# A DRAM-to-DRAM copy of 32 MB on one core: eight transfers of 32 KB per partition, or two of 128 KB

## The chip, the cores and the metric

The kernel runs on one core of a Trainium2 chip. The metric is device time in microseconds (us) from launch to end; the median of several executions is compared. One execution was also recorded by the hardware profiler. Its span is the time from the first to the last instruction of the core, and its device time is a little longer than that span.

## The reference: what is computed

```python
batch, seq, hidden, capacity = 16, 1024, 512, 256
x = np.random.randn(batch, seq, hidden).astype(np.float32)
token_positions = np.random.randint(0, capacity, (batch, seq))

mask = token_positions < capacity
return (x * mask[..., np.newaxis]).astype(np.float32)
```

Rows of `x` (one per token, 512 floats, 2 KB) are kept where the token's position is below the capacity and set to zero elsewhere. The positions are drawn from 0 to 255 and the capacity is 256, so with these inputs every row is kept and the output equals `x`: 16,384 rows, 33.55 MB in and 33.55 MB out.

## The kernel before, in words

The 16,384 rows are seen as 128 groups ("partitions") of 128 consecutive rows each. One partition is 256 KB of consecutive bytes in DRAM, in `x` as in the output.

**The copy.** The kernel copies `x` to the output at once, from DRAM to DRAM, without waiting to know whether a row has to be dropped. The loop at L78 to L83 issues the copy in transfers. Transfer k takes `C` rows of each partition, rows k*C to (k+1)*C, so with C = 16 (L77) there are eight transfers, each with a run of 32 KB from every one of the 128 partitions, 4,096 KB in all. Even k goes to the queue of SP (the SyncE engine), odd k to the queue of ACT (ScalarE). So each queue has four transfers. Each adds 16 to the semaphore `s_copy` when it has landed. No transfer waits for another: the issuing engine only hands it over and goes on.

**The order of issue.** L72 issues a load of the token positions (`tp`, 128 KB, 1 KB per partition) on ACT's queue, ahead of ACT's copies. L86 to L95 take these nine DMA instructions out of the block where they were written and put them ahead of SP's first instruction of the program's first block, so that they are the first thing that SP and ACT do.

**The check beside it.** The positions are 64-bit integers, seen as a low and a high 32-bit half. VectorE (DVE) waits for `tp` (L102), compares the halves (L103 to L115) into a keep flag per row, and adds the flags along each partition (L119). TensorE adds the 128 partial sums with one product with ones (L123). L125 makes one integer of it: 1 if fewer than 16,384 rows are kept. SP, ACT and DVE read that integer into a register (L133) and branch on it.

**The repair.** Within the branch (L141 to L162) the rows would be loaded again, multiplied by the flags and stored, after a wait for all of `s_copy`. With these inputs the integer is 0 and the branch isn't taken.

**The end.** SP, ACT and DVE report to GpSimd (POOL), which clears the semaphores and then waits for the whole copy. That wait, `gp.wait_ge(s_copy, 16 * n_copy)`, with `n_copy` counted by the loop, is the last one of the program.

The functions in full, with the line numbers of the profile:

Of the kernel before, what the change touches and what calls it, by code (L numbers as in the profile page):

```python
# [1 line left out]

# [4 lines left out]


@with_exitstack
def kernel(  # L10
    ctx: ExitStack,
    tc: tile.TileContext,
    x: bass.AP,
    token_positions: bass.AP,
    capacity: bass.AP,
    out: bass.AP,
):
    nc = tc.nc
    P = nc.NUM_PARTITIONS
    fp32 = mybir.dt.float32  # L20
    i32 = mybir.dt.int32
    Alu = mybir.AluOpType

    x_f = x.flatten_outer_dims()
    out_f = out.flatten_outer_dims()
    N, D = x_f.shape
    n_per_p = N // P
    cap = float(int(capacity))
    x_r = x_f.rearrange("(p n) d -> p n d", p=P)
    out_r = out_f.rearrange("(p n) d -> p n d", p=P)  # L30
    tp_i32 = token_positions.rearrange("b s -> (b s)").bitcast(i32)

    sp = nc.sync
    act = nc.scalar
    ve = nc.vector
    pe = nc.tensor
    gp = nc.gpsimd


    tc.close()  # L40
    tc.compile()  # L41

    def sbuf(name, shape, dtype):
        return ctx.enter_context(nc.sbuf_tensor(name, shape, dtype)).ap()

    tp = sbuf("tp", [P, 2 * n_per_p], i32)
    ge = sbuf("ge", [P, n_per_p], fp32)
    lt = sbuf("lt", [P, n_per_p], fp32)
    low = sbuf("low", [P, n_per_p], fp32)
    keep = sbuf("keep", [P, n_per_p], fp32)  # L50
    kept = sbuf("kept", [P, 1], fp32)
    ones = sbuf("ones", [P, 1], fp32)
    drop_i = sbuf("drop_i", [1, 1], i32)
    total = ctx.enter_context(nc.psum_tensor("total", [1, 1], fp32)).ap()
    F = 16
    NBUF = 2
    n_fix = n_per_p // F
    xts = [sbuf(f"xt{b}", [P, F, D], fp32) for b in range(NBUF)]

    s_copy = nc.alloc_semaphore("s_copy")  # L60
    s_tp = nc.alloc_semaphore("s_tp")
    s_ve = nc.alloc_semaphore("s_ve")
    s_pe = nc.alloc_semaphore("s_pe")
    s_ld = [nc.alloc_semaphore(f"s_ld{b}") for b in range(NBUF)]
    s_mul = nc.alloc_semaphore("s_mul")
    s_st = [nc.alloc_semaphore(f"s_st{b}") for b in range(NBUF)]
    s_done = nc.alloc_semaphore("s_done")

    n_copy = 0
    early = []  # L70

    load_tp = act.dma_start(out=tp, in_=tp_i32.rearrange("(p w) -> p w", p=P))  # L72
    early.append(load_tp.then_inc(s_tp, 16).ins)

    C = 16  # L77
    for k in range(n_per_p // C):  # L78
        ins = (sp, act)[k % 2].dma_start(
            out=out_r[:, k * C : (k + 1) * C, :], in_=x_r[:, k * C : (k + 1) * C, :]  # L80
        ).then_inc(s_copy, 16)
        early.append(ins.ins)
        n_copy += 1  # L83


    home = nc.cur_bb.bb  # L86
    first_bb = nc.cur_f.blocks[0]
    first_sp = next(
        k for k, i in enumerate(first_bb.instructions) if i.engine == mybir.EngineType.SP
    )  # L90
    names = [i.name for i in early]
    home.instructions = [i for i in home.instructions if i.name not in names]
    first_bb.instructions = (
        first_bb.instructions[:first_sp] + early + first_bb.instructions[first_sp:]
    )  # L95

    lo = tp[:, 0 : 2 * n_per_p : 2]
    hi = tp[:, 1 : 2 * n_per_p : 2]


    ve.memset(ones, 1.0).then_inc(s_ve, 1)  # L101
    ve.wait_ge(s_tp, 16)  # L102
    ve.tensor_scalar(  # L103
        out=ge, in0=lo, scalar1=0.0, scalar2=None, op0=Alu.is_ge
    ).then_inc(s_ve, 1)
    ve.wait_ge(s_ve, 2)
    ve.scalar_tensor_tensor(  # L107
        out=lt, in0=lo, scalar=cap, in1=ge, op0=Alu.is_lt, op1=Alu.mult
    ).then_inc(s_ve, 1)
    ve.wait_ge(s_ve, 3)  # L110
    ve.scalar_tensor_tensor(  # L111
        out=low, in0=hi, scalar=0.0, in1=lt, op0=Alu.is_equal, op1=Alu.mult
    ).then_inc(s_ve, 1)
    ve.wait_ge(s_ve, 4)
    ve.scalar_tensor_tensor(  # L115
        out=keep, in0=hi, scalar=0.0, in1=low, op0=Alu.is_lt, op1=Alu.add
    ).then_inc(s_ve, 1)
    ve.wait_ge(s_ve, 5)
    ve.tensor_reduce(  # L119
        out=kept, in_=keep, axis=mybir.AxisListType.X, op=Alu.add  # L120
    ).then_inc(s_ve, 1)
    pe.wait_ge(s_ve, 6)
    pe.matmul(out=total, lhsT=ones, rhs=kept, start=True, stop=True).then_inc(s_pe, 1)  # L123
    ve.wait_ge(s_pe, 1)
    ve.tensor_scalar(  # L125
        out=drop_i, in0=total, scalar1=float(N) - 0.5, scalar2=None, op0=Alu.is_lt
    ).then_inc(s_ve, 1)


    for e in (sp, act, ve):  # L130
        e.wait_ge(s_ve, 7)
    ET = mybir.EngineType
    drop = nc.values_load(  # L133
        drop_i[0:1, 0:1],
        engines=[ET.SP, ET.Activation, ET.DVE],
        min_val=0,
        max_val=1,
        skip_runtime_bounds_check_because="a comparison gives 0 or 1",
    )
    with nc.If(drop):  # L140
        for u in range(n_fix):  # L141
            b = u % NBUF
            if u >= NBUF:
                sp.wait_ge(s_st[b], 16 * (u // NBUF))
            sp.dma_start(out=xts[b], in_=x_r[:, u * F : (u + 1) * F, :]).then_inc(s_ld[b], 16)
            ve.wait_ge(s_ld[b], 16 * (u // NBUF + 1))
            for j in range(F):
                c = u * F + j
                ve.tensor_scalar(
                    out=xts[b][:, j, :],  # L150
                    in0=xts[b][:, j, :],
                    scalar1=keep[:, c : c + 1],
                    scalar2=None,
                    op0=Alu.mult,
                ).then_inc(s_mul, 1)
            if u == 0:
                act.wait_ge(s_copy, 16 * n_copy)
            act.wait_ge(s_mul, (u + 1) * F)
            act.dma_start(out=out_r[:, u * F : (u + 1) * F, :], in_=xts[b]).then_inc(s_st[b], 16)
        for b in range(NBUF):  # L160
            act.wait_ge(s_st[b], 16 * (n_fix // NBUF))


    for e in (sp, act, ve):
        e.sem_inc(s_done, 1)
    gp.wait_ge(s_done, 3)
    own = [s_tp, s_ve, s_pe, *s_ld, s_mul, *s_st, s_done]
    ids = sorted(s.num for s in own)
    assert ids == list(range(ids[0], ids[-1] + 1))
    gp.sem_clear(range(ids[0], ids[-1] + 1))  # L170
    gp.wait_ge(s_copy, 16 * n_copy)
    gp.sem_inc(s_copy, -16 * n_copy)


# [1 line left out]
_INS = ['x', 'token_positions', 'capacity']  # L176
_OUTS = [((16, 1024, 512), 'float32')]

_NUMBERS = {'capacity': 256}


# [26 lines left out]
```

## Time and profile before

| What | Value |
|---|---|
| median of 4 runs | 105.22 us (104.95 to 105.36) |
| device time of the profiled execution | 105.01 us |
| its span | 103.1 us |
| device time around the span (105.01 - 103.1) | 1.9 us |
| DVE busy | 1.5 us, 7 instructions |
| PE busy | 0.2 us |
| POOL busy | 0.2 us |
| last instruction of the check (L125) starts | 6.49 us |
| issue of SP's four copies | 0.0 to 3.0 us |
| issue of ACT's load and four copies | 0.13 to 3.3 us |

How to read the profile of this kernel: issuing a DMA, waiting for a semaphore and branching aren't counted as busy time, so an engine whose row is empty may be issuing or waiting. The work is in the DMA rows. "DMA" is the mean busy share of the core's 16 DMA engines, in tenths for each of 40 slices of the span. "GB/s" counts the bytes of the packets that begin in a slice, so with large packets it swings from slice to slice although the flow is even. Bytes are counted once, on their way from source to destination; the line on HBM (the DRAM) counts reads and writes apart. A packet is one piece of a transfer that one DMA engine carries. The queue q1 is SP's and q10 is ACT's (it also carries the `tp` load).

### The profile page before, as it was taken

To read this page: it belongs to the slowest core of one execution; us is meant where nothing else is said; L and a number is where in the kernel's file an instruction comes from. 1 tells how busy PE (TensorE), PEld (TensorE's weight loads), DVE (VectorE), ACT (ScalarE), POOL (GpSimd) and SP (SyncE) were. 2 spreads that over 40 slices of the span, in tenths; PEclk is the share of its full clock that TensorE was granted. 3 is DMA by queue.
4 is the path that set the end of the run, shared out by engine and by line. 5 is a ranking of instruction groups with operands and counts; after the bars stand their busy time and mean duration, and the time that the engine had idled before them with its cause. 6 is when DMAs were issued, how large, how long until landed. Compare 5 with 4: busy or idle time off the path is not lost. (4 is left out here: it accounts for less than half of the span.)

```text
span 103.1 us, 70 instructions
## 1 busy us (share of the span) xinstructions
PE 0.2 (0%) x2; PEld 0.1 (0%) x2; DVE 1.5 (1%) x7; POOL 0.2 (0%) x4
## 2 busy tenths in 40 slices
PE   0000000000000000000000000000000000000000
PEld 0000000000000000000000000000000000000000
DVE  0140000000000000000000000000000000000000
POOL 0000000000000000000000000000000000000000
DMA  7998999989989999799798999898997998998974
GB/s 254 407 381 292 330 283 330 343 292 369 343 292 394 305 318 407 254 356 356 254 407 305 305 407 318 292 369 292 356 356 254 407 330 280 369 343 305 394 254 165
DMA packets 1297, 33.69 MB, mean 327 GB/s; under 512 B 144, under 2 KB 272, under 8 KB 272
## 3 DMA queue, kind: packets, MB, share of 16 engines
q10 hardware_dynamic: 720, 16.91, 49.5%
q1 hardware_dynamic: 576, 16.78, 48.2%
q14 instruction: 1, 0.01, 0.0%
HBM read 33.69 MB, written 33.55 MB: 652 GB/s over the span
## 5 line engine op out<-in xcount | busy, mean ns | idle before, releaser
L115 DVE SCALAR_TENSOR_TENSOR keep<-tp,low 128x128 f32<-128x128 int32 x1 | 0.3, 292 | 0.0
L107 DVE SCALAR_TENSOR_TENSOR lt<-tp,ge 128x128 f32<-128x128 int32 x1 | 0.3, 291 | 0.0
L111 DVE SCALAR_TENSOR_TENSOR low<-tp,lt 128x128 f32<-128x128 int32 x1 | 0.3, 291 | 0.0
L119 DVE TENSOR_REDUCE kept<-keep 128x1 f32<-128x128 f32 x1 | 0.3, 286 | 0.0
L103 DVE TENSOR_SCALAR ge<-tp 128x128 f32<-128x128 int32 x1 | 0.2, 227 | 0.0
L123 PE MATMUL total<-kept,ones 128*1 128x1 f32 x2 | 0.2, 164 | 6.3 <-DVE kept L119 6.3
L125 DVE TENSOR_SCALAR drop_i<-total 1x1 int32<-1x1 f32 x1 | 0.1, 145 | 0.3 <-PE total L123 0.3
L101 DVE MEMSET ones<- 128x1 f32 x1 | 0.1, 59 | 4.7 <-PEq L41 4.7
L189 POOL MEMSET const-bfloat16-1.0<- 128x1 bf16 x1 | 0.1, 101 | 0.0
L189 POOL MEMSET const-uint8-127<- 128x1 uint8 x1 | 0.1, 101 | 0.0
L189 POOL MEMSET const-float32-0.0<- 128x1 f32 x1 | 0.1, 98 | 0.2 <-issue 0.2
L189 POOL MEMSET const-float32-1.0<- 128x1 f32 x1 | 0.1, 98 | 0.0
L123 PEld LDWEIGHTS total<-kept,ones 128*1 128x1 f32 x2 | 0.1, 80 | 6.3 <-DVE kept L119 6.3
## 6 DMA issues: line engine op xcount, KB each, us to landing
out_dram<-in_x_dram SPq DMA_DIRECT2D x4, 4096.0 KB, 61.5
out_dram<-in_x_dram ACTq DMA_DIRECT2D x4, 4096.0 KB, 67.2
tp<-in_token_positions_dram ACTq DMA_DIRECT2D x1, 128.0 KB, 2.1
```

The lines of the kernel that those rows point to most:

```text
L101: ve.memset(ones, 1.0).then_inc(s_ve, 1)
L103: ve.tensor_scalar(out=ge, in0=lo, scalar1=0.0, scalar2=None, op0=Alu.is_ge).then_inc(s_ve, 1)
L107: ve.scalar_tensor_tensor(out=lt, in0=lo, scalar=cap, in1=ge, op0=Alu.is_lt, op1=Alu.mult).then_inc(s_ve, 1)
L111: ve.scalar_tensor_tensor(out=low, in0=hi, scalar=0.0, in1=lt, op0=Alu.is_equal, op1=Alu.mult).then_inc(s_ve, 1)
L115: ve.scalar_tensor_tensor(out=keep, in0=hi, scalar=0.0, in1=low, op0=Alu.is_lt, op1=Alu.add).then_inc(s_ve, 1)
L119: ve.tensor_reduce(out=kept, in_=keep, axis=mybir.AxisListType.X, op=Alu.add).then_inc(s_ve, 1)
L123: pe.matmul(out=total, lhsT=ones, rhs=kept, start=True, stop=True).then_inc(s_pe, 1)
L125: ve.tensor_scalar(out=drop_i, in0=total, scalar1=float(N) - 0.5, scalar2=None, op0=Alu.is_lt).then_inc(s_ve, 1)
L189: nc = _bacc.Bacc("TRN2", target_bir_lowering=False, num_devices=1)
```

## The change

The constant `C` becomes 64. The loop then makes two transfers instead of eight: SP copies rows 0 to 63 of every partition and ACT rows 64 to 127, so that each transfer takes 128 KB of each partition's 256 KB, 16,384 KB in all. `n_copy` becomes 2, and the waits on `s_copy` are for 32 instead of 128.

```diff
-    C = 16
+    C = 64
     for k in range(n_per_p // C):
         ins = (sp, act)[k % 2].dma_start(
             out=out_r[:, k * C : (k + 1) * C, :], in_=x_r[:, k * C : (k + 1) * C, :]
```

In the built program a transfer of before is 128 runs of 8,192 floats (32 KB). A transfer of the changed kernel is 128 times 2 runs of 16,384 floats (64 KB): the 128 KB of a partition are cut in two. Every other instruction, and the order of all of them on PE, DVE and POOL, is the same; on SP and ACT one copy instruction stands where four stood.

## The prediction

> **What bounds the kernel now.** I read the page's engine rows first, then its DMA rows, then the chain, then the time windows, and at last the DMA view of the two ends.
>
> ```profile
> span 103.1 us, 70 instructions
> PE 0.2 (0%) x2; PEld 0.1 (0%) x2; DVE 1.5 (1%) x7; POOL 0.2 (0%) x4
> ...
> DMA  7998999989989999799798999898997998998974
> ...
> DMA packets 1297, 33.69 MB, mean 327 GB/s; under 512 B 144, under 2 KB 272, under 8 KB 272
> ## 3 DMA queue, kind: packets, MB, share of 16 engines
> q10 hardware_dynamic: 720, 16.91, 49.5%
> q1 hardware_dynamic: 576, 16.78, 48.2%
> ...
> HBM read 33.69 MB, written 33.55 MB: 652 GB/s over the span
> ## 4 chain that ended last, share of the span: by engine, by line
> DVE 2%; issue 0%; PE 0%
> ```
>
> No engine computes for more than 1.5 us, and the DMA row is near nine tenths from the first slice to the last but two. The chain names only the check (2% of the span): it ends in the first 7 us, and the copy, which really ends last, isn't in it because its end is a semaphore and no instruction. So the copy is the bound. The packets tell how it is cut: eight copies of 128 pieces plus 16 completion packets, the `tp` load the same, and one for instructions: 9 x 144 + 1 = 1297. Per queue, 576 = 4 x 144. The two shares add up to 97.7%, or 100.7 of 103.1 us: the 16 DMA engines hardly ever rest.
>
> ```profile
> 1.60:102.70 101.10, 0.19 (x2) 0.09 (x2) 1.53 (x7) 0.00 (x0) 1.00 0.99 333
> ...
> 6.00:26.00 20.00, 0.19 (x2) 0.09 (x2) 0.36 (x2) 0.00 (x0) 1.00 0.99 326
> 26.00:46.00 20.00, 0.00 (x0) 0.00 (x0) 0.00 (x0) 0.00 (x0) 1.00 1.01 338
> 46.00:66.00 20.00, 0.00 (x0) 0.00 (x0) 0.00 (x0) 0.00 (x0) 1.00 0.99 329
> 66.00:86.00 20.00, 0.00 (x0) 0.00 (x0) 0.00 (x0) 0.00 (x0) 1.00 0.99 329
> ```
>
> The last two numbers of each window are the DMA share and GB/s. Between the first piece of the copy (1.6 us; in the DMA view one packet of q1 begins just before 1.62) and its end (102.7 us) the engines are 99% busy at 333 GB/s, and every 20 us look alike. A busy engine isn't an engine at full speed, though, as the start shows:
>
> ```profile
> DMA packets 120, 1.63 MB, mean 400 GB/s; under 512 B 16, under 2 KB 72, under 8 KB 72
> q1 hardware_dynamic: 48, 1.57, 103.2%
> q10 hardware_dynamic: 72, 0.06, 4.2%
> ```
>
> That is the DMA view from 1.6 to 5.68 us: 48 pieces of the copy, three per engine, all from SP's queue. 1.57 MB in 4.08 us is 385 GB/s. So the same engines with the same pieces have gone 16% faster than their mean; what holds them to 333 GB/s later is outside of them, most likely the memory that they all read and write (652 GB/s both ways over the span). The Trainium skill, page "HBM Reference", section "Specifications (TRN2)", gives about 716 GB/s for a domain's DRAM; by that the copy's 67.1 MB would need at least an estimated 93.7 us in whatever pieces, and no run here shows that limit.
>
> **The change part by part.**
>
> 1. *Pace of the copy: 0.* The bytes, the 16 engines, the two queues and the 256 KB pitch of the partitions stay. The pieces become 64 KB, and the two queues work 128 KB apart in a partition instead of 32 KB. Which addresses are open at one time is thus new, and no row shows its price. Bounds from the 20 us windows: at 326 GB/s all through, 101.1 x 333/326 is 103.3 us, +2.2; at 338 it is 99.6, -1.5. Part of that spread is counting (a round of 16 pieces is 0.52 MB, 26 GB/s of a window). I take 0, the mean.
>
> 2. *Gaps between packets: -0.1.* Each engine has 64 copy pieces and 8 completion packets; it will have 32 and 2. 72 packets become 34. The engines' idle time within the 101.1 us is 1% at most, 1.0 us, and 0.4 us of that is the uneven end (part 4). The rest, 0.6 us, is 8 ns per packet; 38 packets fewer would give -0.3 us, if the engines and not the memory set the pace. Bounds 0 and -0.3; I take -0.1.
>
> 3. *Start: +0.3.* The issue instructions:
>
> ```profile
> L79 SPq DMA_DIRECT2D out_dram<-in_x_dram x4: 582/626/1045, 0.0 to 2.4; - x4
> L79 ACTq DMA_DIRECT2D out_dram<-in_x_dram x4: 581/638/791, 0.6 to 2.5; - x4
> ```
>
> (ns, shortest, median, longest; then first and last start.) SP's first issue, of 128 pieces, starts at 0.0; data flows at 1.6. The one issue now has 256 pieces. If issue time doesn't depend on their number, nothing changes; if it doubles and the data waits for all of it, the cost is +1.05 us, the longest row. The `tp` load has 128 pieces as well and took 393 ns (timeline), so the number of pieces isn't all; I take +0.3, half of a median issue. The six issues that go are worth nothing: they run from 0.6 to 3.3 us, beside data that is already flowing. The `tp` load is still first on ACT's queue; if a 64 KB piece got ahead of it, the check would end some 3 us later than now (one piece at 20.8 GB/s per engine, 333/16, is 3.15 us). It ends at 6.6 us, so 96 us of copy cover that. The branch and POOL's last wait stay as they are.
>
> 4. *End: 0.* The 16 completion packets of ACT's last transfer all lie between 101.9 and 102.8 us in the DMA view: the engines end within some 0.8 us of each other. Each still carries 2 MB. While some have ended, the rest have the memory to themselves and may speed up, as at the start. Bounds: 0, and +1.6 if one engine ends half a new piece (32 KB, 1.57 us) late.
>
> *Semaphores: 0.* Six fewer completions; nobody waits for the single ones, only POOL for the sum.
>
> Sum against the profiled execution: 105.01 + 0 - 0.1 + 0.3 + 0 = 105.2. That execution is 0.2 below the median of 105.22, so on the median the forecast is **105.4 us**, no change that a measurement of this kernel could tell (about 0.3%, or 0.3 us).
>
> A rule that speaks against this change is in the Trainium skill, page "Perfetto Trace Analysis", section "DMA Optimizations": smaller transfers may let some begin sooner. By that the start term would stand at its upper end, and the sum at about 106.0 instead of 105.2; the trace shows only that 1.6 us pass before the first data and can't say how much of it goes with the number of pieces.
>
> **The rivals.**
>
> - *The end frays (slower): 106.2 to 107.0.* An engine can't hand a piece to another. With pieces twice as long the engines may end twice as far apart: +0.8 us, up to +1.6 with one engine half a piece late. For it: the last two slices already fall to 7 and 4 tenths, and in the last 4 us only ACT's queue has work, so nothing fills gaps. Against: every engine has the same 2 MB, and the late ones may speed up. It decides from the point where the spread of the 16 last completions exceeds about 1.2 us.
> - *The memory likes the new addresses less (slower): 106.5 to 107.6.* Half or all of +2.2 from part 1. For it: the pace already varies between 385 and 326 GB/s with nothing but addresses and engine phases changing. Against: the 20 us windows, between which the transfers move through the whole partition, differ by few per cent.
> - *The fast start lasts longer, or the pace is better (faster): 103.9 to 104.8.* The first three pieces per engine came from SP's queue alone, at 385 GB/s. Three pieces of 64 KB would take twice as long; if they keep that pace, the second half gains 4.08 x (385/333 - 1) = 0.6 us: 104.8. With the better pace of part 1 instead, 105.4 - 1.5 = 103.9. Against: from 97.9 to 101.4 us ACT's queue is alone too, at 328 GB/s in the window, so being alone isn't what made the start fast.
> - *Nothing changes in what the engines see*, if pieces are cut to 32 KB again on the way: the forecast's own time.
>
> **How the numbers follow.** Forecast (with the last rival): 0.38. Fraying end 0.20, worse addresses 0.17: together 0.37 slower. Faster: 0.25, since the start shows that there is pace to be had, but nothing in the change reaches for it. The range takes in the bounds of the rivals, 103.9 to 107.6; some 0.15 is left out, for two costs that come together and for prices that no row shows. The forecast's own range is 104.9 to 105.5.
>
> **What would show it.** Packets: 2 x (256 + 16) + 144 + 1 = 689, q1 with 272 and q10 with 416; more means that the pieces are cut again. The start: the first q1 packet at about 1.9 us instead of 1.6. Pace: 333 GB/s within 1% in the long windows; 326 or less is the address rival. End: a spread of the last 16 completions of about 0.8 us; over 1.2 is the fraying end. The fast start: pieces of q1 alone from 1.6 to about 10 us at over 370 GB/s would be the faster rival. The forecast is wrong if the pace moves by more than 1%, since each per cent is 1.0 us and every other term is below that.

## The result and the profile after

The changed kernel takes 105.51 us (median of 44 runs, 105.08 to 106.1) against 105.12 us before (70 runs, 104.66 to 105.73). The ratio is 1.0039, with a 95% interval of 1.003 to 1.0049: slower by 0.4 us. The profiled execution took 105.6 us with a span of 103.7; that of before took 105.01 with 103.1.

The page of the changed kernel, in the lines that answer to those shown of before:

```profile
span 103.7 us, 64 instructions
...
DMA  9994999859999759999399999299994899992990
...
DMA packets 689, 33.69 MB, mean 325 GB/s; under 512 B 48, under 2 KB 176, under 8 KB 176
## 3 DMA queue, kind: packets, MB, share of 16 engines
q10 hardware_dynamic: 416, 16.91, 49.2%
q1 hardware_dynamic: 272, 16.78, 48.6%
...
HBM read 33.69 MB, written 33.55 MB: 648 GB/s over the span
```

The packets are the 689, 272 and 416 that two transfers in 64 KB pieces give, so nothing cuts the pieces again. The two shares add up to 97.8%, as before within a tenth: of the longer span that is 101.4 us busy, against 100.7. The time isn't in gaps between packets (2.3 us of rest against 2.4); the same bytes keep the engines busy 0.7 us longer. The low digits in the DMA row come from counting: a packet is put down to the slice in which it begins, and a piece of 64 KB now lasts longer than a slice (about 2.9 us in the first pieces, against 2.6).

The time windows of before (first fence) and after (second fence), last two numbers DMA share and GB/s:

```profile
1.50:7.20 5.70, 0.19 (x2) 0.09 (x2) 1.53 (x7) 0.00 (x0) 1.00 1.06 390
...
30.00:60.00 30.00, 0.00 (x0) 0.00 (x0) 0.00 (x0) 0.00 (x0) 1.00 1.00 333
60.00:90.00 30.00, 0.00 (x0) 0.00 (x0) 0.00 (x0) 0.00 (x0) 1.00 1.00 331
```

```profile
1.50:7.20 5.70, 0.19 (x2) 0.09 (x2) 1.54 (x7) 0.00 (x0) 1.00 1.07 385
...
30.00:60.00 30.00, 0.00 (x0) 0.00 (x0) 0.00 (x0) 0.00 (x0) 1.00 0.99 330
60.00:90.00 30.00, 0.00 (x0) 0.00 (x0) 0.00 (x0) 0.00 (x0) 1.00 1.00 330
```

No stretch stands out. A difference of 1 to 3 GB/s is below what such a window can show: one round of 16 pieces of 64 KB is 1.05 MB, 35 GB/s of a 30 us window. So windows of one trace cannot place 0.4 us, and the experiments have to.

Issue of the copies, in the changed kernel (ns, shortest, median, longest):

```profile
L79 SPq DMA_DIRECT2D out_dram<-in_x_dram x1: 694/694/694, 0.0 to 0.0; - x1
L79 ACTq DMA_DIRECT2D out_dram<-in_x_dram x1: 643/643/643, 0.6 to 0.6; - x1
```

SP's issue of 256 pieces took 694 ns. Before, its first issue of 128 pieces took 619 ns (the longest, 1045 ns, was its third), and in e2 and e8 below one issue of 512 and one of 2,048 pieces took 617 ns each. The number of pieces isn't what an issue costs.

### The profile page after: what moved, and what is told of

The parts are those of the page before. It is cut to its first block, busy times and chain, and to the rows that moved or that the text cites. A ratio compares the mean times of both kernels' runs of the same rounds, so it can differ in the third digit from the quotient of the medians.

```text
span 103.7 us, 64 instructions
## 1 busy us (share of the span) xinstructions
PE 0.2 (0%) x2; PEld 0.1 (0%) x2; DVE 1.5 (1%) x7; POOL 0.2 (0%) x4
## 6 DMA issues: line engine op xcount, KB each, us to landing
out_dram<-in_x_dram ACTq DMA_DIRECT2D x1, 103.1
```

## The experiments

Each kernel is compared with before on its own chip, where before had a median of 106.35 us (first four runs), 106.40 us (next four) or 105.16 us (last four). Ratios are to before, as recorded; they are not quite the quotients of the medians. The diffs are against the changed kernel unless said otherwise.

**First question: the size of the pieces, the number of transfers, or the end?** Theory P puts the cost on pieces of 64 KB, theory N on having two transfers only, theory F on engines that end further apart when the pieces are long.

Run e1, four transfers in 64 KB pieces:

```diff
-    C = 64
+    C = 32
```

> C = 32: four transfers, two on each queue, in pieces of 64 KB. Theory P (the pieces of 64 KB cost the time, however many transfers they are in) expects the changed kernel's time, ratio to before about 1.004, and the 16 last completions spread over about 1.0 us. Theory N (what costs is that two transfers alone remain, each walking through half a partition before it goes on to the next) expects a ratio of 1.000 to 1.002.

Measured: 106.75 us, ratio 1.0028 (1.0004 to 1.0051). The trace has 721 packets, and the 16 last completions lie 1.0 us apart.

Run e2, two transfers in 32 KB pieces:

```diff
-    C = 64
+    C = 16
+    xq = x_r.rearrange("p (h q c) d -> p q h (c d)", q=2, c=C)
+    oq = out_r.rearrange("p (h q c) d -> p q h (c d)", q=2, c=C)
+    for q, e in enumerate((sp, act)):
+        ins = e.dma_start(out=oq[:, q], in_=xq[:, q]).then_inc(s_copy, 16)
```

(In place of the loop over k; the last two lines of that loop stay. SP takes the even 32 KB of a partition, ACT the odd ones.)

> Two transfers, one on each queue, in pieces of 32 KB: SP takes the even 32 KB of every partition and ACT the odd ones. Theory P (piece size) expects the time of before, ratio 1.000, and 0.8 us of spread at the end. Theory N (two transfers, partition by partition) expects 1.004.

Measured: 106.44 us, ratio 1.0002 (0.9973 to 1.003), and a spread of 1.17 us at the end. Two transfers as such cost nothing that can be seen, and four in long pieces are slower: this speaks for P and against N, although the two intervals overlap (the medians are 0.31 us apart). The spread was expected at 0.8 us and is larger than the changed kernel's 1.05, without a longer time. That is the first mark against F. The changed kernel's spread is read from the view of 102.28 to 103.34 us, which just holds its 16 completion packets:

```profile
DMA packets 16, 0.00 MB, mean 0 GB/s; under 512 B 16, under 2 KB 16, under 8 KB 16
q10 hardware_dynamic: 16, 0.00, 0.8%
```

One thing goes with the size of the pieces in these runs and wasn't taken apart from it: how far apart in a partition the two queues work. It is 32 KB in before and in e2, 64 KB in e1 and 128 KB in the changed kernel.

Run e3, small pieces at the end:

```diff
+    for e, n in [(sp, 64), (act, 48), (act, 4), (act, 4), (act, 4), (act, 4)]:
```

> As the changed kernel, but ACT's half ends in small pieces: 48 rows in one transfer, then four transfers of 4 rows (8 KB pieces). Theory F (the loss is at the end, where engines with long pieces end further apart) expects 0.3 to 0.4 us back, ratio about 1.000 to 1.001, and a spread of the last completions of about 0.8 us or less. If the spread has nothing to do with the size of the last pieces, 1.004 and about 1.0 us.

Measured: 106.69 us, ratio 1.003 (1.0006 to 1.0054). The 16 completions lie within 0.88 us, and nothing is gained. The views from 103.65 to 104.54 us and from 104 us on show all 16 completions, and that four engines had theirs before 104:

```profile
DMA packets 31, 0.12 MB, mean 138 GB/s; under 512 B 16, under 2 KB 16, under 8 KB 16
```

```profile
DMA packets 16, 0.03 MB, mean 55 GB/s; under 512 B 12, under 2 KB 12, under 8 KB 12
```

Run e4, the same end on the kernel before:

```diff
+    for e, n in [(sp, 16), (act, 16), (sp, 16), (act, 16), (sp, 16), (act, 16), (sp, 16), (act, 4), (act, 4), (act, 4), (act, 4)]:
```

> As before (pieces of 32 KB), but the last 16 rows on ACT go in four transfers of 4 rows (8 KB pieces). Theory F expects the end to fray less here too: 0.2 to 0.4 us faster than before, ratio 0.996 to 0.998. If the spread at the end is not set by the pieces, 1.000.

Measured: 106.57 us, ratio 1.0017 (0.999 to 1.0043): no gain. But the completions still lie 0.82 us apart, against 0.77 before, so the small pieces didn't make the engines end together, and this run doesn't test F. Against F stand e2, with a wide end and no loss, and e3, which ends nearly as evenly as before and stays slow. What a quite even end would be worth, no run shows.

**Second question: is it lost at every piece, or once per launch?** Two runs make the copy four times (three times to spare tensors), so what is lost per megabyte counts four times and what is lost at the two ends counts once. Both have the same code, e5 with `C = 16` and e6 with `C = 64`:

```diff
+    spare = [
+        nc.dram_tensor(f"spare{r}", [N, D], fp32).ap().rearrange("(p n) d -> p n d", p=P)
+        for r in range(3)
+    ]
+    for to in [*spare, out_r]:
+        # ... the loop over k, with `to` in place of `out_r`
```

> The copy of before (C = 16) made four times, three times to spare DRAM tensors and then to the output: four times the bytes behind one start and one end. It is the base of the next run. Every theory expects 105.1 + 3 x 101 = some 408 us if the pace of the copy stays, about 3.88 times before.

> The copy of the changed kernel (C = 64) made four times in the same way. Theory PACE (with pieces of 64 KB every megabyte takes about 0.3 to 0.4% longer) expects 1.2 to 1.7 us over the run with 32 KB. Theory ENDS (the start and the end cost the 0.4 us, once) expects 0.3 to 0.5 us over it.

Measured: 412.57 us (412.1 to 413.36, 6 runs) with 32 KB, 413.03 us (412.39 to 413.87) with 64 KB. The difference of the medians is 0.46 us, about what one copy loses, and below the 1.2 to 1.7 that PACE asked for. It isn't sharp: the ranges overlap, and drawing anew from the six runs of each gives a 95% interval of about -0.3 to 1.2 us. The windows from 20 to 400 us of the two traces, 32 KB first:

```profile
20.00:400.00 380.00, 0.19 (x2) 0.09 (x2) 1.54 (x7) 0.00 (x0) 1.00 1.00 328
```

```profile
20.00:400.00 380.00, 0.00 (x0) 0.00 (x0) 0.00 (x0) 0.00 (x0) 1.00 1.00 328
```

In the long middle the pace is the same, 328 GB/s. These windows count a packet where it begins, and a round of pieces of 64 KB can be worth 2.8 GB/s in them, more than the 1.0 to 1.3 GB/s that PACE asks for. With the bytes of each packet spread over the packet's time, the same windows give 328.5 and 328.6 GB/s. So the middle loses nothing by the piece, and PACE is refuted in these two executions. Where the 0.4 us goes they can't show, as they took the same time altogether (412.97 and 412.94 us).

**Third question: are shorter pieces better still?** Run e7:

```diff
-    C = 64
+    C = 8
```

> C = 8: sixteen transfers, eight on each queue, pieces of 16 KB. If the pace falls steadily with the size of a piece, half the size gains what double the size lost: ratio 0.996 to 0.998. If 64 KB is past a bend and smaller pieces are alike, 1.000 within 0.2%. If the packets' own overhead counts, 1.003 or more.

Measured: 106.9 us, ratio 1.0043 (1.0019 to 1.0068). Run e8 is e2 with `C = 4`:

> Two transfers as in the run with two transfers of 32 KB pieces, but in pieces of 8 KB (SP every even 8 KB, ACT every odd). Steady fall of the pace with piece size: 0.993 to 0.997. Pieces below 64 KB alike: 1.000. Overhead per packet (192 more per engine than with 32 KB, some ns each): up to 1.01.

Measured: 106.82 us, ratio 1.0045 (1.0015 to 1.0076). Both are slower, so "the longer the piece, the slower" is wrong. Of the sizes tried in one size throughout, 32 KB is best, and 16 KB lose as much as 64. Why the shorter ones lose, no run shows.

**Fourth question: which end?** Four runs side by side: the changed kernel again, its end undone, its start undone, and both. The plans of the last three, in the order of issue:

```diff
+    # e10: for e, n in [(sp, 64), (act, 32), (act, 16), (act, 16)]:
+    # e11: for e, n in [(sp, 16), (act, 64), (sp, 16), (sp, 32)]:
+    # e12: for e, n in [(sp, 16), (act, 32), (sp, 16), (act, 16), (sp, 32), (act, 16)]:
```

Transfers of 16 rows have pieces of 32 KB, those of 32 and 64 rows have pieces of 64 KB.

> The changed kernel once more, beside the three below, on their chip. All theories: ratio 1.003 to 1.005. Its trace gives a second look at the two ends: if the 1.05 us between the first and the last completion belongs to pieces of 64 KB, it comes again (0.9 to 1.2); if it was chance, it can be 0.7.

> The changed kernel with only the end undone: ACT's 64 rows go as 32 (64 KB pieces) and twice 16 (32 KB pieces), so that the last 25 us of ACT's queue are as before. Theory END (all of the fixed 0.4 us comes from the long pieces at the end) expects 1.000 to 1.001; theory START expects 1.004 still; no place at all (a small loss of pace all along) expects about 1.003.

> The changed kernel with only the start undone: SP's 64 rows go as twice 16 (32 KB pieces), then 32 (64 KB pieces); ACT as changed. Theory START (the first pieces, at 361 GB/s instead of 400, and the later first piece cost it) expects 1.000 to 1.001; theory END expects 1.004; loss all along expects about 1.003.

> Both ends undone, the middle in 64 KB pieces: SP 16, 16, 32 rows, ACT 32, 16, 16. If the cost sits at the two ends, whichever: 1.000. If it is a loss of pace all along: about 1.002, half the bytes being in 64 KB pieces.

| Run | First pieces (SP) | Last pieces alone | Median | Ratio (95%) | Spread of last completions |
|---|---|---|---|---|---|
| e9, changed again | 64 KB | 64 KB, ACT | 105.51 | 1.004 (1.0018 to 1.0062) | 1.01 us |
| e10, end undone | 64 KB | 32 KB, ACT | 105.44 | 1.0021 (1.0004 to 1.0038) | 0.90 us |
| e11, start undone | 32 KB | 64 KB, SP | 105.25 | 1.0007 (0.9992 to 1.0022) | 0.69 us |
| e12, both undone | 32 KB | 32 KB, ACT | 104.87 | 0.9973 (0.9954 to 0.9992) | 0.98 us |

The loss comes again in e9. With the start alone undone, the kernel is back within the noise of before, as START expected (1.000 to 1.001); that is 0.25 us less than e9, and the two intervals just touch. The end alone gives back less than END expected, and its interval overlaps most of that of e9. With both undone the loss is gone, though half of the bytes still go in 64 KB pieces; a loss of pace all along (about 1.002 expected) doesn't fit. The spread is no guide: e11 ends in pieces of 64 KB and has the smallest one.

e12 is faster than both kernels, by 0.27% of before. No theory expected that, and its cause is open.

The kept traces can be asked about START too. Five of the kernels with one copy begin on SP's queue with pieces of 32 KB (before, e2, e4, e11, e12) and five with 64 KB (changed, e1, e3, e9, e10); the chips of e1 to e4 and of e9 to e12 are spread evenly. With the bytes of each packet spread over its time, the copy had come so far (mean of five traces, lowest to highest):

| | begins with 32 KB | begins with 64 KB |
|---|---|---|
| by 5 us | 1.17 MB (1.15 to 1.19) | 1.14 MB (1.08 to 1.16) |
| by 10 us | 2.91 MB (2.85 to 2.94) | 2.80 MB (2.70 to 2.90) |
| by 20 us | 6.10 MB (6.01 to 6.19) | 6.01 MB (5.86 to 6.09) |
| pace from 20 to 95 us | 331.2 GB/s (327.8 to 333.5) | 331.0 GB/s (328.5 to 333.8) |
| end of the copy | 103.4 us (102.7 to 104.2) | 103.7 us (103.0 to 104.5) |

The 0.10 MB that the second group is behind at 10 us is 0.3 us of copying. At 20 us it is still that, the pace from there on is the same, and the copy ends 0.3 us later. So in these traces about the whole loss is there by 10 us, which speaks for START. Each is one execution, and the groups overlap, so it isn't proof. The distance between the queues is 32 KB at the start of every kernel of the first group, and 64 or 128 KB in the second, so this doesn't part the two either.

The plans with mixed pieces differ from the others in one more thing, which e11's DMA view from 6 to 32 us shows (packets, MB, share):

```profile
DMA packets 171, 8.53 MB, mean 328 GB/s; under 512 B 0, under 2 KB 0, under 8 KB 0
## 3 DMA queue, kind: packets, MB, share of 16 engines
q10 hardware_dynamic: 90, 5.90, 68.0%
q1 hardware_dynamic: 80, 2.62, 30.9%
```

The engines took about as many pieces from each queue, 90 and 80, as if in turn. While SP has pieces of 32 KB and ACT of 64, ACT's queue gets 2.3 times the bytes. So the division of the pieces also decides when a queue runs dry. In e11 ACT's last piece ends at 77.4 us, and the DMA view from 80.5 to 102.1 us has SP's alone:

```profile
DMA packets 96, 6.29 MB, mean 291 GB/s; under 512 B 0, under 2 KB 0, under 8 KB 0
## 3 DMA queue, kind: packets, MB, share of 16 engines
q1 hardware_dynamic: 96, 6.29, 88.4%
```

In e12 SP's last piece ends at 97.8 us and ACT's at 102.9, much as in before (98.0 and 102.7). In e10 SP's queue is done at 86.6 us. The runs on the ends thus change the balance of the queues too. In the first 10 us the balance can't matter yet, since neither queue is near its end; what it adds to e10, e11 and e12 later stays open.

## Why the prediction was right or wrong

The time was right: 105.4 forecast, 105.51 measured, well within 103.9 to 107.6. "Within 0.3%" was the likeliest case, and at 0.39% (0.30 to 0.49) the kernel lies just past that line on the slow side. The sum had +0.2 us and the runs of the result have +0.4. What carried the forecast, a pace that stays, was right; that the memory holds it, as the prediction supposed, no run shows. That the two small terms came within 0.2 us was luck: the start cost something for another reason than the one it was priced by, and no run shows the gain from the gaps.

- *Pace, 0.* Right for the middle, where it mattered most: 328 GB/s with either size over 380 us. The case "the memory likes the new addresses less", at 1 us or more, is refuted, as is a better pace. The 20 us windows of before, from which I took +2.2 and -1.5 us, showed mostly the counting of pieces: with the bytes spread over the packets' time, 20 to 50 and 50 to 80 us of before give 333.5 and 333.4 GB/s.
- *Gaps, -0.1.* Nothing in the times can tell it; the engines' rest went from 2.4 to 2.3 us.
- *Start, +0.3.* The reason failed: "if it doubles and the data waits for all of it". An issue doesn't grow with its pieces (694 ns for 256; 617 ns for 2,048 in e8), the 1045 ns of the upper bound were not a first issue, and the first data came at 1.73 us, or 1.53 us when the kernel was profiled again, around the 1.61 of before. The sign fits all the same, and by the table of the traces the size too: 0.3 us behind by 10 us, and with the start in 32 KB pieces 105.51 becomes 105.25 us. What in the first pieces costs it isn't the issue and isn't the moment of the first byte. What it is, no run shows.
- *End, 0, and the rival of the fraying end.* The spread grew as that rival said, from 0.77 to 1.05 and 1.01 us, and stayed below the 1.2 from which it was to decide. As a mechanism it has nothing for it: e2 has a spread of 1.17 us and the time of before, e3 comes down to 0.88 us and stays slow.
- *Hidden work.* Right. The check ended at 4.5 us, sooner than the 6.6 of before and not later; the copy ran to 103.3 us.
- *The rival of the longer fast start.* Its premise came true in part, its gain didn't. The DMA view of the changed kernel from 1.72 to 7.25 us:

```profile
DMA packets 69, 2.12 MB, mean 383 GB/s; under 512 B 16, under 2 KB 37, under 8 KB 37
## 3 DMA queue, kind: packets, MB, share of 16 engines
q1 hardware_dynamic: 32, 2.10, 105.3%
q10 hardware_dynamic: 37, 0.02, 1.3%
```

SP's queue was alone with two pieces per engine, not three. Being alone lasted 1.4 us longer, and nothing came of it: before carried 1.98 MB of the copy by 7.2 us and the changed kernel 1.95, although ACT's queue had joined in before. The pace of this start was also read too high, since the views count whole the pieces that begin in them. The shares tell: before's 1.57 MB took 103.2% of 4.08 us, which is 373 GB/s instead of 385, or 12% above the mean and not 16%. The changed kernel's 2.10 MB took 105.3% of 5.53 us, 360 GB/s. Even so, 373 GB/s is 746 read and written, above the 716 from which the prediction worked out its floor of 93.7 us; so this trace doesn't bear out that figure as a limit on the copy, and why it doesn't is open.

The step that was mis-sized is the start with its reason: +0.3 less the 0.1 of the gaps stood in the sum, and +0.4 was measured. The rule of smaller transfers that begin sooner, from the Trainium skill's page "Perfetto Trace Analysis", section "DMA Optimizations", has no run for it here: the first data of the changed kernel came later in one trace and sooner in the other, and two transfers in 32 KB pieces (e2) took the time of eight. The page gives the gain for DMA engines that are generally idle, and here they were busy for 97.7% of the span.

## What to carry to other kernels

When a copy keeps every DMA engine busy, cutting it into fewer, larger transfers may move the time by no more than tenths of a per cent, as here. In these runs the loss went with the size of the pieces, not with the number of transfers, and it showed at the first pieces and not in the middle. To tell a loss per byte from a loss per launch, do the same work four times in one launch and compare the differences, with more runs than the six here when the loss is smaller than their scatter. Two queues share the engines piece by piece, so with unequal pieces the one with the short ones falls behind. No run here shows that this costs time: e11, where one queue was dry from 77.4 us on, took the time of before.

Read a spread of ends from one mark per engine. The last 16 pieces aren't the last piece of each of 16 engines when the pieces are short.

## What the runs showed of the hardware

- The issue of a copy on SP or ACT took 0.57 to 0.70 us in most cases (single ones up to 1.05), with 128, 256, 512 or 2,048 pieces alike.
- A queue takes a limited number of transfers ahead. In e5 (sixteen transfers of 128 pieces on each queue) SP issued nine in 0.6 to 0.8 us each, and the tenth took 34 us. ACT's tenth, with the `tp` load as its first, took 15 us. SP's row (ns, shortest, median, longest):

```profile
L84 SPq DMA_DIRECT2D spare<-in_x_dram x10: 582/609/33974, 0.0 to 6.1; - x10
```

- The engines shared pieces, not bytes, between two queues: 90 pieces (5.90 MB) to 80 (2.62 MB) in e11.
- The copy starts faster than it goes on. With the bytes spread over the packets' time, it ran at 360 to 374 GB/s from 2 to 7.2 us in before, changed, e5 and e6, and at 328 to 333 from 20 us to 95 us (to 400 in e5 and e6), with pieces of 32 or 64 KB. With SP's queue alone it held the same pace, 332 GB/s from 78 to 100 us in e11. What ends the faster stretch is open.
